# Moving the tiles that TensorE reads by 1 KB in SBUF: a decoder layer in split float32 on one core

## The chip, the cores and the metric

The kernel runs on one core of one Trainium2 chip. The metric is the device time of one execution in microseconds, taken as the median of several runs. The engines are called as in the profile: PE is TensorE's matmul stream, PEld its weight loads (LDWEIGHTS), DVE is VectorE, ACT is ScalarE, POOL is GpSimd, and SP issues the DMAs.

## The reference

One decoder layer over 512 tokens of width 2048, in float32. Three token mixers run on the same normalised input, their outputs go through one output projection, and a SwiGLU feed-forward follows. Each has a residual add, and a last RMSNorm ends it. What matters here is the second half:

```python
x = x + jnp.concatenate([ya, yb, yc], axis=-1) @ w_out[l]
h = rmsnorm(x, ffn_norm[l])
x = x + (jax.nn.silu(h @ w_gate[l]) * (h @ w_up[l])) @ w_down[l]   # 2048 -> 5632 -> 2048
return rmsnorm(x, final_norm)
```

## The kernel before

**Split operands.** Every large product is made in the fp32r type with both operands split into a high part (`hi`, a rounded copy) and a low part (`lo`, the rest). A product of two such operands is three matmuls (`mm3`, line 292): high by high, high by low, low by high. A matmul has a stationary operand of 128 columns, which LDWEIGHTS loads, and a moving operand of 256 or 512 columns (1 or 2 KB in each partition).

**Phase 1** (up to about 970 us) makes the input projection and the three mixers. Its matmul groups carry the names of their PSUM tiles: `pf`, `pq`, `pig`, `pvs`, `pcq`, `pk` and so on are projections; the rest is attention and the gated recurrence. `po` and `pp` are the output projection.

**Phase 2** begins with the last columns of the output projection, whose weights stay resident in `wo` tiles (groups `bt<-wo,mT`). Then comes the feed-forward: 44 chunks (22 of gate and 22 of up columns, 256 columns each). Each chunk is made by a scheme of seven products, `P1` to `P7`, each of 8 steps, and a step is two matmuls (lines 1337 and 1338). The high weights meet 512 moving columns, and the low weights meet 256:

```python
mm(ps, hi[:, q], v.rearrange("p k h t -> p (k h t)"), first and q == 0, False, skip_group_check=True)
mm(ps[:, :256], lo[:, q], v[:, 0, 0], False, q == 7, skip_group_check=True)
```

In the trace a product shows as 16 matmuls that alternate, for instance `Xg<-A,w` (512 columns) and `Xg<-A,lo` (256). The moving tile is `A` for P1 and P4 (groups X) and P2 (group V), and `S` for the others: P5 uses S1 and P3 uses S4 (both in group Z), P6 uses S2 and P7 uses S3 (both in group X, so `Xg<-S` and `Xu<-S` are always S2 or S3). From the second block on, each chunk also carries a piece of the down projection of the block before: four steps of 12 matmuls (`fd<-w,aT`, 512 columns), put between the products by line 1449:

```python
ORDER = ("P1", "d", "P5", "d", "P6", "P2", "d", "P7", "d", "P4", "d", "P3")
```

40 of the 44 chunks have such `d` steps (39 in this order, the last one in a similar one). The kernel ends with the last piece of the down projection, `bt<-wl`.

**Places in SBUF.** Tiles come from pools that lie one behind the other in each partition, in the order of lines 117 to 121 and 1113: `const`, `big`, `slots`, `raws`, `rings`, and then `cb`, `ysp`, `wk` in phase 1, in whose place `fp` lies in phase 2. The sizes in `const` decide where all that follows begins, and `fp` began with the 64 bytes of `s4`. Counted from the start of a 2 KB block, the built program puts them here:

```
tiles                                                   before   after
big, slots, rings: hT, mT, A11 A12 A22 S1, S4, aT, w      160     1184   (moved by 1024)
fp: wo, S2, S3, lo (the low weights)                      224     1184   (moved by  960)
fp: xq, hf (not read by a large product)                  480     1440   (moved by  960)
ysp: w0, split inputs of the attention                   1088       64   (moved by 1024)
const: ident                                             1152     1152
```

All sizes of these tiles are multiples of 2 KB or 4 KB, so a 512-column moving operand always begins at the place in the table; a stationary operand of 512 bytes begins there or 512, 1024 or 1536 bytes further. Where a `w` tile holds two row blocks of 256 columns (`pf`, `pvs`), the second one begins 1024 bytes further.

Of the kernel before, what the change touches and what calls it, by code (L numbers as in the profile page):

```python
# [31 lines left out]
F32 = mybir.dt.float32  # L32
# [8 lines left out]
P = 128  # L41
T = 512
NT = T // P
# [64 lines left out]
def tile_hymba(ctx: ExitStack, tc: tile.TileContext, x, attn_norm, w_in, q1, k1, q2, k2, da_norm, hg_norm,  # L108
# [8 lines left out]
    const = ctx.enter_context(tc.tile_pool(name="const", bufs=1))  # L117
# [8 lines left out]
    def slot(name):  # L126
        return slots.tile([P, 1024], F32, name=name, tag="slot")
# [64 lines left out]
    sp.dma_start(ident, ctab[:, C_ID:C_ID + P])  # L192
    mhalf = const.tile([P, 4], F32, name="mhalf")
    pool.memset(mhalf, -0.5)

    def rstd_of(dst, ss, n, dim):

        pool.tensor_scalar(dst, ss, 1.0 / dim, EPS, op0=ALU.mult, op1=ALU.add)
        pool.tensor_tensor(dst, dst, mhalf[:, :n], op=ALU.pow)
# [911 lines left out]
    with ExitStack() as p2:  # L1111
        hurry[0] = False
        fp = p2.enter_context(tc.tile_pool(name="fp", bufs=1))
        s4 = fp.tile([P, NT, 4], F32, name="s4")
        gain2 = [slot(f"gain2{hf}") for hf in range(2)]
        for hf in range(2):
            sp.dma_start(gain2[hf], bcast_row(ffn_norm[0:1, hf * 1024:(hf + 1) * 1024], 1024))
# [418 lines left out]
```

## Time and profile before

| | |
|---|---|
| time, median of 3 runs | 2404.65 us (2404.49 to 2404.81) |
| time of the profiled execution | 2403.6 us |
| its span, first to last instruction | 2401.8 us |
| mean granted TensorE clock | 0.997 |

The span is what the views of the trace cover; the profiled execution took 1.8 us more than its span, and 1.05 us less than the median. The records of consecutive matmuls overlap, since a matmul drains while the next one streams. So the duration in a record (some 390 ns for 512 columns) is not what a matmul costs; its cost is the time from its start to the next start.

### The profile page before, as it was taken

The page shows a single profiled execution, that of the slowest core. Times are in us where ns is not written, and L with a number is a line of the kernel's source. Part 1 is how long each engine was busy: PE and PEld are TensorE (multiplying, and loading weights), DVE is VectorE, ACT ScalarE, POOL GpSimd, SP SyncE. Part 2 cuts the span into 40 slices and gives each one's busy share as a digit, 9 for nine tenths or more (in the row PEclk, how much of TensorE's full clock was granted, in tenths as well). Part 3 has the DMA queues.
Part 4 walks back from the last instruction along what each step waited for, and adds up shares of the span by engine and source line. Part 5 has one row for each costly group of instructions (what it writes and reads, how often), then busy time and mean ns, then how long its engine had stood idle before and what let it go on. Part 6 is the DMA issues. An engine that isn't in the chain of part 4 may idle for free.

```text
span 2401.8 us, 32892 instructions
## 1 busy us (share of the span) xinstructions
PE 2361.2 (98%) x12720; PEld 2019.1 (84%) x12720; DVE 1584.2 (66%) x2472; ACT 1032.5 (43%) x1800; POOL 50.3 (2%) x85
## 2 busy tenths in 40 slices
PE   9999999999999999979999999999999999999998
PEld 7898888898888778768888888888888888888887
DVE  6355556543656574687777777777777777777785
ACT  5343443443434443454444444444444444444452
POOL 2000000000000000000000000000000000000001
PEclk9999999999999999999999999999999999999999
DMA  6322222443221422534555555565555555555553
GB/s 207 97 73 80 65 82 81 137 131 100 62 62 53 144 81 74 179 101 122 191 187 190 190 190 193 193 193 193 193 193 193 191 187 188 188 193 192 189 187 150
DMA packets 355888, 354.17 MB, mean 147 GB/s; under 512 B 12882, under 2 KB 286738, under 8 KB 355732
## 3 DMA queue, kind: packets, MB, share of 16 engines
q1 hardware_dynamic: 355732, 352.07, 45.9%
q8 instruction: 100, 1.64, 0.3%
q14 instruction: 56, 0.46, 0.1%
HBM read 302.74 MB, written 49.28 MB: 147 GB/s over the span
## 4 chain that ended last, share of the span: by engine, by line
PE 94%; DVE 3%; ACT 1%; DMA 1%; issue 1%; POOL 0%; SPq 0%; ACTq 0%; POOLq 0%; DVEq 0%
PE fd L145 18%; PE Xu L145 10%; PE Xg L145 10%; PE pig L145 6%; PE po L145 5%; PE Zg L145 5%; PE Zu L145 5%; PE pq L145 3%; PE pf L145 3%; PE pcq L145 3%; PE Vg L145 2%; PE Vu L145 2%; PE bt L145 2%; PE pak L145 2%; PE pk L145 2%; PE sc L145 2%
## 5 line engine op out<-in xcount | busy, mean ns | idle before, releaser
L202 ACT ACTIVATE w<-raw 128x512 fp32r<-128x512 f32 (+2 forms) x698 | 549.0, 790 | 926.7 <-PE fd L145 148.4
L203 DVE TENSOR_TENSOR w<-raw,w 128x512 fp32r<-128x512 f32 (+1 forms) x432 | 293.8, 681 | 343.5 <-ACT w L202 340.4
L145 PE MATMUL fd<-w,aT 128*128 128x512 f32 x1920 | 467.6, 392 | 0.0
L203 DVE TENSOR_TENSOR lo<-raw,w 128x1024 fp32r<-128x1024 f32 x266 | 323.3, 1223 | 179.0 <-ACT w L202 179.0
L145 PEld LDWEIGHTS fd<-w,aT 128*128 128x128 f32 x1920 | 348.9, 188 | 75.3
L1260 DVE TENSOR_TENSOR raw<-raw,raw 128x1024 f32<-128x1024 f32 x134 | 163.4, 1219 | 6.8 <-DMA raw<-in_w_gate_dram 3.2
L145 PE MATMUL pig<-w,hT 128*128 128x512 f32 x576 | 138.3, 395 | 0.0
L145 PE MATMUL po<-w,mT 128*128 128x512 f32 x576 | 136.1, 393 | 0.0
L145 PE MATMUL Xu<-A,w 128*128 128x512 f32 x352 | 125.7, 396 | 1.5 <-DVE C L1346 1.5
L145 PE MATMUL Xg<-A,w 128*128 128x512 f32 x352 | 125.6, 396 | 1.3 <-DVE C L1346 1.3
L145 PE MATMUL Zg<-S,w 128*128 128x512 f32 x352 | 124.2, 392 | 1.7 <-DVE S L1233 1.7
L145 PEld LDWEIGHTS po<-w,mT 128*128 128x128 f32 x576 | 106.8, 188 | 21.5
L145 PEld LDWEIGHTS pig<-w,hT 128*128 128x128 f32 x576 | 106.2, 188 | 21.3
L145 PE MATMUL Zu<-S,w 128*128 128x512 f32 x352 | 124.2, 392 | 0.0
L145 PE MATMUL Xu<-S,w 128*128 128x512 f32 x352 | 123.0, 391 | 0.6 <-ACT C L1343 0.6
L145 PE MATMUL Xg<-S,w 128*128 128x512 f32 x352 | 122.8, 390 | 0.0
L1403 DVE TENSOR_TENSOR xq<-xq,fd 128x512 f32<-128x512 f32 x156 | 100.1, 683 | 0.3
L145 PE MATMUL Xg<-A,lo 128*128 128x256 f32 x352 | 99.1, 281 | 0.0
L145 PE MATMUL Xu<-A,lo 128*128 128x256 f32 x352 | 99.1, 281 | 0.0
L145 PE MATMUL Zg<-S,lo 128*128 128x256 f32 x352 | 98.4, 280 | 0.0
L145 PE MATMUL Zu<-S,lo 128*128 128x256 f32 x352 | 98.4, 280 | 0.0
L145 PE MATMUL Xg<-S,lo 128*128 128x256 f32 x352 | 97.6, 277 | 0.0
(344 smaller groups left out, 4324.8 us busy)
## 6 DMA issues: line engine op xcount, KB each, us to landing
raw<-in_w_gate_dram SPq DMA_DIRECT2D x112, 512.0 KB, 4.6
raw<-in_w_up_dram SPq DMA_DIRECT2D x112, 512.0 KB, 4.6
raw<-in_w_down_dram SPq DMA_DIRECT2D x88, 512.0 KB, 5.2
raw<-in_w_in_dram SPq DMA_DIRECT2D x80, 512.0 KB, 3.5
xq<-y SPq DMA_DIRECT2D x78, 512.0 KB, 4.9
y<-xq SPq DMA_DIRECT2D x78, 512.0 KB, 2.7
raw<-in_w_out_dram SPq DMA_DIRECT2D x32, 512.0 KB, 3.6
raw<-in_w_in_dram SPq DMA_DIRECT2D x48, 256.0 KB, 3.1
```

The source lines that it names most:

```text
L145: return pe.matmul(o, l, r, start=start, stop=stop, **kw)
L202: act.activation(hi, src, AF.Copy)
L203: dve.tensor_tensor(lo, src, hi.bitcast(F32), op=ALU.subtract)
L1260: dve.tensor_tensor(self.raw[out], self.raw[a], self.raw[b], op=ALU.subtract)
L1403: dve.tensor_tensor(o, o, ps[tt], op=ALU.add)
```

## The change

`s4`, which the squares of the rows are summed into, is taken from the pool `const` and no longer from `fp`, and a tile of 960 bytes that nothing uses is added to `const`. `const` grows by 64 + 960 = 1024 bytes, and the tiles move as in the table above. The built program has the same instructions in the same order on every engine, with the same semaphores and the same values waited for. Only addresses differ.

```diff
@@ -192,6 +192,9 @@
     sp.dma_start(ident, ctab[:, C_ID:C_ID + P])
     mhalf = const.tile([P, 4], F32, name="mhalf")
     pool.memset(mhalf, -0.5)
+    s4 = const.tile([P, NT, 4], F32, name="s4")
+
+    const.tile([P, 240], F32, name="room")
 
     def rstd_of(dst, ss, n, dim):
 
@@ -1111,7 +1114,6 @@
     with ExitStack() as p2:
         hurry[0] = False
         fp = p2.enter_context(tc.tile_pool(name="fp", bufs=1))
-        s4 = fp.tile([P, NT, 4], F32, name="s4")
         gain2 = [slot(f"gain2{hf}") for hf in range(2)]
```

## Rows read from the trace of the kernel before

**Rows 1.** The page: busy time, granted clock by slice, the chain by engine.

```profile
PE 2361.2 (98%) x12720; PEld 2019.1 (84%) x12720; DVE 1584.2 (66%) x2472; ACT 1032.5 (43%) x1800; POOL 50.3 (2%) x85
...
PEclk9999999999999999999999999999999999999999
...
PE 94%; DVE 3%; ACT 1%; DMA 1%; issue 1%; POOL 0%; SPq 0%; ACTq 0%; POOLq 0%; DVEq 0%
```

**Rows 2.** Waits of PE: total us, times, longest us.

```profile
PE hpsA L1225 <- DVE A L1233: 7.8, 3, 3.2
PE hpsS L1225 <- DVE S L1233: 6.1, 3, 3.8
PE pt L962 <- DVE pr L930: 4.0, 3, 1.8
```

**Rows 3.** Chain in order of time, one chunk: start us, us, matmuls.

```profile
1506.23 2.77 PE fd L145 x12
1509.00 2.74 PE Xg L145 x16
1511.74 2.78 PE Vg L145 x16
1514.52 2.77 PE fd L145 x12
1517.29 2.74 PE Xg L145 x16
1520.03 2.74 PE fd L145 x12
1522.78 2.77 PE Xg L145 x16
1525.55 2.77 PE Zg L145 x16
1528.32 2.77 PE Xu L145 x16
1531.09 2.77 PE fd L145 x12
...
1561.49 0.70 PE fd L145 x3
```

**Rows 4.** Busy time by engine in that chunk, PE clock, DMA share, GB/s.

```profile
1500.50:1530.90 30.40, 30.40 (x162) 26.10 (x161) 23.15 (x28) 13.71 (x18) 0.00 (x0) 1.00 0.59 191
```

**Rows 5.** Chain, a 512-column stage of phase 1.

```profile
69.93 43.52 PE pig L145 x192
```

**Rows 6.** Chain, the kernel's last stage.

```profile
2349.91 43.53 PE bt L145 x192
```

**Rows 7.** Chain, a 256-column stage of phase 1.

```profile
471.78 5.74 PE pvs L145 x48
```

**Rows 8.** Timeline, PE: an earlier 256-column stage, and what follows it.

```profile
42.05 5.91 PE L145 MATMUL pf<-w,hT 128*128 128x256 f32 x48
47.80 0.40 PE L145 MATMUL pq<-hT,w 128*128 128x512 f32 x1
```

**Rows 9.** Timeline, PE: steps of a product with S2.

```profile
1510.22 0.39 PE L145 MATMUL Xg<-S,w 128*128 128x512 f32 x1
1510.45 0.28 PE L145 MATMUL Xg<-S,lo 128*128 128x256 f32 x1
1510.56 0.39 PE L145 MATMUL Xg<-S,w 128*128 128x512 f32 x1
```

**Rows 10.** Timeline, PEld: the weight loads in a product's first steps.

```profile
1503.30 0.19 PEld L145 LDWEIGHTS Zg<-S,lo 128*128 128x128 f32 x1
1503.53 0.19 PEld L145 LDWEIGHTS Zg<-S,w 128*128 128x128 f32 x1
```

**Rows 11.** Timeline, PE: the matmuls of the same two steps.

```profile
1503.30 0.39 PE L145 MATMUL Zg<-S,w 128*128 128x512 f32 x1
1503.53 0.28 PE L145 MATMUL Zg<-S,lo 128*128 128x256 f32 x1
```

**Rows 12.** Timeline, PE: output projection with resident weights, and what follows.

```profile
997.30 14.68 PE L145 MATMUL bt<-wo,mT 128*128 128x512 f32 x63 [1.28 <-issue]
1011.82 1.03 PE L1225 MATMUL hpsA<-ident,hf 128*128 128x128 f32 x8
```

**Rows 13.** Chain, products of the first block, behind a stall.

```profile
1085.32 2.83 PE Zg L145 x16
1088.14 2.83 PE Zu L145 x16
1090.97 2.83 PE Xg L145 x16
1093.80 2.83 PE Zg L145 x16
1096.62 2.80 PE Xg L145 x16
```

## Prediction

> **What bounds the kernel now.** I read the page first: PE is busy for 98% of the span, the chain that ended last is PE for 94%, and the clock stands at its upper level (2.4 GHz) in every slice [rows 1]. Then the waits: the longest total that PE waited for anything is 7.8 us [rows 2]. So the time is, nearly, the sum of the steps from one matmul's start to the next. Since the change leaves order, semaphores and shapes alone, it can act only through the length of such a step. The view for that is the chain in order of time, which gives whole runs of equal matmuls. In the feed-forward it shows nothing but PE, eleven pieces for a chunk: seven products and four `fd` pieces. From the first `fd` piece of one chunk to that of the next it is 1561.49 - 1531.09 = 30.40 us [rows 3], and PE is busy for all of such a window [rows 4].
>
> The reader should see that these pieces are not equal. A product has 16 matmuls, eight of each width. It takes 2.77 us with A and in group Z, and 2.74 us where `Xg` stands behind an `fd` piece for P6 and P7, which read S2 and S3. The `fd` pieces take 2.77 us, except 2.74 us behind the second of these [rows 3]. Shape, clock and cover are the same; what differs is the place of the tiles: S2 and S3 begin at 224, the A tiles, S1 and S4 at 160. So place does count here, by about 1%.
>
> How can it? A weight load starts together with the matmul ahead of it: the load for `Zg<-S,lo` starts at 1503.30 with the matmul `Zg<-S,w`, and the next load at 1503.53 with the matmul `Zg<-S,lo` [rows 10, 11]. So two reads of SBUF run at once, a moving operand and the following weights, and I take it (it is not shown) that they disturb each other by the distance between their places. In S2 and S3 steps that distance is 224 to 224 in the 512-column matmul and 224 to 160 in the 256-column one; in the others it is 160 to 224 and 160 to 160.
>
> The Trainium skill says otherwise ("TensorE: Matmul & The Clock Gate", Step-by-step: what each phase is for): "Loading the next tile's weights doesn't steal SBUF read bandwidth from the running matmul." By that sentence addresses cannot matter and the change is worth 0. The trace does not agree with it in full: 2.74 against 2.77 us for matmuls of the same shapes [rows 3].
>
> **The change part by part.** The removed and added lines issue no instruction of their own; `s4` keeps its writers and readers. What is left is two moves.
>
> *The shift by 1 KB that all share.* It leaves every distance between `big`, `slots` and `rings` as it was. What it could alter is where an operand crosses a 2 KB boundary. For weights the trace has the answer: a stage's four token tiles load from 160, 672, 1184 and 1696 in turn, the last one across the boundary; after the change the same four places come in another order. For 256 moving columns too: in `pvs` every second group of 12 begins at 160 and at 1184, and a matmul takes 5.74/48 = 119.6 ns [rows 7]; in the `pf` stage three quarters begin at 1088 or 64, the rest at 160, and it takes (47.80 - 42.05)/48 = 119.8 ns [rows 8]. I price this move at 0. Moving operands of 512 columns at 1184 are in no row; that stays a rival below. Other engines and DMA move with their tiles; in the chunk DVE is busy for 23.15 and ACT for 13.71 of 30.40 us, and DMA for 0.59 [rows 4], so even some per cent there stay hidden.
>
> *The shift by 960 bytes of the `fp` tiles.* It brings S2, S3, `wo` and `lo` to the same place as the rest. All pairs then are 1184 to 1184. Stages in which all operands already stand alike give the price: 512 columns take 43.52/192 = 226.7 ns in `pig` and 43.53/192 = 226.7 ns in the last stage [rows 5, 6], 256 columns take 119.6 ns [rows 7]. Eight steps of one each are 8 x 346.3 ns = 2.77 us. That is what products with A, S1 and S4 take now, so I leave these at 2.77. The others follow:
> - S2 and S3 products: 2.74 to 2.77, two in a chunk: +0.06 us.
> - the `fd` piece behind the second one: 2.74 to 2.77: +0.03 us.
> - `Vg<-A` behind the first one, now 2.78 [rows 3], to 2.77: -0.01 us.
> - that is +0.08 us in a chunk, and 40 chunks have it: +3.2 us. The four chunks of the first block have eight such products without `fd`: 8 x 0.03 = +0.2 us.
> - `bt<-wo` has 224 against 160 now: (1011.82 - 997.30)/63 = 230.5 ns [rows 12]. With all alike 226.7 ns; 96 of them: -0.4 us.
>
> Sum: +3.0 us. The profiled execution took 2403.6 us, 2401.8 of it span, and 1.05 us less than the median of the runs; with the sum it becomes 2406.6 us, and against the median 2407.7 us, +0.12%.
>
> The pair of a 512-column step and a 256-column step in one place is in no row, so both ends are kept. Low end: each step as short as the shortest steady one. A step pair of S2 takes 1510.56 - 1510.22 = 0.34 us [rows 9], eight are 2.72 us; twelve `fd` matmuls at 226.7 ns are 2.72 us. Eleven pieces of 2.72 are 29.92 against 30.40 us [rows 4]: -0.48 us, in 40 chunks -19.2 us. High end: right behind a stall in the first block, products with the very same tiles ran at 2.83 us, four in a row [rows 13]. So a pair can settle at more than one length. Seven products at 2.83 and four `fd` pieces at 2.77 are 30.89 us: +0.49 us, in 40 chunks +19.6 us. I take the value between, since the stages with one place are nearest to the new state, and since it is what most products show now.
>
> **The rivals.**
> - *All pairs fall into the short step* (faster). For it: both steady 512-column stages with one place, 226.7 ns, have the length that S2's steps have too, and `fd` pieces would then enter in step and lose their 2.77. Against it: 256 columns in one place take 119.6 ns, where S2's 256-column step takes 1510.56 - 1510.45 = 0.11 us [rows 9]. -19.2 us: 2385.5 us.
> - *All pairs settle in the long step* (slower). For it: rows 13 show it, and the first `fd` matmuls behind a product with one place are those that make that piece longer than 12 x 226.7 ns = 2.72 us. Against it: it came only behind a stall, and the chain shows 2.77 for the same tiles 40 chunks long. It decides if the load of `lo`, now moved from 64 bytes beside the moving operand to its very place, costs the 512-column step 7 ns more. +19.6 us: 2424.3 us.
> - *Nothing changes at all* (same). Then the 2.74 us would come from the order of the products and not from places. For it: P6 and P7 always stand behind `fd` in the chain. Against it: so does P4, with 2.77 [rows 3]. 2404.7 us. The sentence of the Trainium skill quoted above would have this outcome.
> - *The 2 KB boundary counts for 512 columns*, which the operand now crosses at its column 216 and not 472. If it costs or saves one such step of 6.7 ns (the difference of 2.77 and 2.72 over eight pairs), the program's 7500 matmuls with 512 columns make 50 us either way: 2455 or 2354 us. No row speaks for it; rows 7 and 8 speak against.
>
> **How the numbers follow.** My forecast 0.42; all short 0.16; all long 0.19; nothing 0.10; boundary 0.03 faster and 0.04 slower; the rest, 0.06, is a mixture of product kinds with half of either end. A measurement of this kernel tells about 0.2% (4.8 us) from no change. The forecast, 2404 to 2411 us in its own range, lies within that for nine parts in ten; with "nothing changes" this makes same 0.38 + 0.10 = 0.48. Faster: 0.16 + 0.03 + 0.03 = 0.22. Slower: 0.19 + 0.04 + 0.03 + 0.04 = 0.30. The range takes in both ends of the pair and leaves out the boundary: 2385 to 2425 us.
>
> **What would show it.** In the chain of the changed kernel: `Xg<-S` at 2.77 us and the `fd` behind it at 2.77; `Vg<-A` at 2.77; `pig` and the last stage at 43.5 us; `pvs` at 119.6 ns; `bt<-wo` at 226.7 ns. If A products leave 2.77, the pair settles elsewhere, and it should do so in all seven products of a chunk and in all chunks alike. If `pig` or the last stage leave 43.5 us, the common shift by 1 KB counts, and my first price is wrong.

## Result, and the profile of the changed kernel

The changed kernel takes 2420.66 us (median of 4 runs, 2415.63 to 2423.57) against 2404.57 us (4 runs). The ratio is 1.0064, 95% interval 1.0049 to 1.0078: slower by 0.64%, or 16 us. The profiled execution is the quickest of the four, 2415.63 us with a span of 2413.8 us.

The page (busy time, granted clock by slice, the chain by engine) and the waits of PE (total us, times, longest us) answer to [rows 1, 2]:

```profile
PE 2375.0 (98%) x12720; PEld 2020.3 (84%) x12720; DVE 1584.8 (66%) x2472; ACT 1031.2 (43%) x1800; POOL 50.8 (2%) x85
...
PEclk9999999999999999999999999999999999999999
...
PE 94%; DVE 3%; ACT 1%; DMA 1%; issue 1%; POOL 1%; SPq 0%; ACTq 0%; POOLq 0%; DVEq 0%
```

```profile
PE hpsS L1227 <- DVE S L1235: 6.0, 3, 3.8
```

PE has 13.8 us more busy time in the same 12,720 matmuls, in a span that is 12.0 us longer. The longest total wait is 6.0 us, where it was 7.8. So the time lies in the steps themselves. The chain in order of time (start us, us, matmuls), first the stages of phase 1, then one chunk, then the last stage:

```profile
69.76 43.52 PE pig L145 x192
...
471.60 5.74 PE pvs L145 x48
...
1533.92 2.73 PE fd L145 x12
...
1539.46 2.78 PE fd L145 x12
1542.24 2.81 PE Xu L145 x16
1545.05 2.83 PE Vu L145 x16
1547.88 2.75 PE fd L145 x12
...
1553.44 2.78 PE fd L145 x12
...
1564.69 2.73 PE fd L145 x12
...
2361.93 43.53 PE bt L145 x192
```

`pig`, `pvs` and the last stage take as long as they did, to the hundredth [rows 5 to 7]. In a chunk every product is longer: 2.81 us behind an `fd` piece and 2.83 us behind another product, where it was 2.74 to 2.78 [rows 3]. The four `fd` pieces went both ways, 2.73 to 2.78 where they were 2.74 or 2.77, and their sum stays, 11.04 us for 11.05. The chunk takes 1564.69 - 1533.92 = 30.77 us against 30.40: +0.37 us, in 40 chunks +14.8 us (counting all of them as equal to this one). Over it the clock is full and PE is never idle (columns as in [rows 4]):

```profile
1533.92:1564.69 30.77, 30.77 (x161) 26.14 (x161) 21.74 (x27) 12.62 (x16) 0.00 (x0) 1.00 0.57 187
```

The timeline of PE shows a product with S2 again, to set against [rows 9]:

```profile
1511.99 0.40 PE L145 MATMUL Xg<-S,w 128*128 128x512 f32 x1
...
1513.05 0.40 PE L145 MATMUL Xg<-S,w 128*128 128x512 f32 x1
```

The two starts are three pairs apart, which take 1513.05 - 1511.99 = 1.06 us, 0.353 us each, where a pair with S2 took 0.34. From the same view, `bt<-wo` takes (1009.12 - 994.73)/63 = 228.4 ns a step [rows 12]:

```profile
994.73 14.55 PE L145 MATMUL bt<-wo,mT 128*128 128x512 f32 x63 [0.49 <-issue]
1009.12 1.03 PE L1227 MATMUL hpsA<-ident,hf 128*128 128x128 f32 x8
```

### The profile page after: what moved, and what is told of

Its sections match the earlier page's. It is cut to its first block, busy times and chain, and to the rows that moved or that the text cites. A ratio compares the mean times of both kernels' runs of the same rounds, so it can differ in the third digit from the quotient of the medians.

```text
span 2413.8 us, 32892 instructions
## 1 busy us (share of the span) xinstructions
PE 2375.0 (98%) x12720; PEld 2020.3 (84%) x12720; DVE 1584.8 (66%) x2472; ACT 1031.2 (43%) x1800; POOL 50.8 (2%) x85
## 4 chain that ended last, share of the span: by engine, by line
PE 94%; DVE 3%; ACT 1%; DMA 1%; issue 1%; POOL 1%; SPq 0%; ACTq 0%; POOLq 0%; DVEq 0%
PE fd L145 18%; PE Xu L145 10%; PE Xg L145 10%; PE pig L145 5%; PE po L145 5%; PE Zg L145 5%; PE Zu L145 5%; PE pq L145 3%; PE pcq L145 3%; PE Vg L145 3%; PE Vu L145 2%; PE pf L145 2%; PE bt L145 2%; PE pak L145 2%; PE pk L145 2%; PE sc L145 2%
## 5 line engine op out<-in xcount | busy, mean ns | idle before, releaser
L145 PE MATMUL Xu<-S,lo 128*128 128x256 f32 x352 | 98.7, 280 | 0.0
```

What stands on the lines that cost most here:

```text
L145: return pe.matmul(o, l, r, start=start, stop=stop, **kw)
```

## Experiments

Two theories. **Distance:** a step's length depends on how far, within a block of 512 bytes, the moving operand lies from the weights loaded meanwhile; the change took the distance of `lo`, S2 and S3 to zero. **Place:** the shift by 1 KB that all tiles share does it. In the edits, P is 128 and a float32 column is 4 bytes, so a pad of 112 columns is 448 bytes and one of 16 columns is 64. Where a run is compared with the kernel before, that ran on the same chip. Chunk lengths are taken from the first `fd` piece of an up chunk to that of the next chunk, as above.

### The distance alone, and the shift alone

`e1_no_room` is the changed kernel without the room, so all tiles stand at 224 in a 512-byte block:

```diff
     s4 = const.tile([P, NT, 4], F32, name="s4")
-    const.tile([P, 240], F32, name="room")
```

> Only the distance is closed, without the shift by 1 KB: s4 moves to the first pool and nothing else is added, so hi, lo, the residuals' tiles and all other operands start 224 bytes into a 512-byte block. Theory 'distance' (the bytes between the start of what streams and of what is loaded next, within 512 bytes, set the pace): products of a chunk at 2.81 us behind fd and 2.83 us behind another product, as in the changed kernel, time 2415 to 2424 us. Theory 'place' (the shift by 1 KB does it): products stay at 2.77 and 2.74 us, time 2404.6 us.

`e2_room_only` is the kernel before with 1,024 bytes of room; `s4` stays in `fp`:

```diff
     pool.memset(mhalf, -0.5)
+    const.tile([P, 256], F32, name="room")
```

> Only the shift by 1 KB, without closing the distance: 1,024 bytes of room in the first pool, s4 stays where it was, so everything is moved by 1,024 bytes and lo, S2 and S3 stay 64 bytes beside hi. Theory 'distance': as the kernel before, A, S1 and S4 products 2.77 us, S2 and S3 products 2.74 us, time within 0.1% of 2404.6 us. Theory 'place': products 2.81 to 2.83 us, time 2415 to 2424 us.

Measured: `e1_no_room` 2421.55 us against 2404.56, ratio 1.0070 (1.0058 to 1.0083); `e2_room_only` 2403.59 us, ratio 0.9998 (0.9989 to 1.0007). The chain of each, first without the room, then with the room alone:

```profile
1536.38 2.83 PE Xu L145 x16
1539.21 2.73 PE fd L145 x12
...
1569.98 0.23 PE fd L145
```

```profile
1533.70 2.77 PE fd L145 x12
...
1542.01 2.74 PE Xu L145 x16
...
1564.11 2.77 PE fd L145 x12
```

The chunk takes 1569.98 - 1539.21 = 30.77 us without the room and 1564.11 - 1533.70 = 30.41 us with the shift alone. The whole effect comes with the distance. The shift by 1 KB is worth nothing that can be seen here (0.11% at the most, either way), and so is the crossing of a 2 KB boundary by a 512-column operand: the A tiles, S1, S4 and the `w` tiles cross it at the same column as in the changed kernel. Nor does a common shift by 64 bytes count: within 512 bytes all these tiles stand at 224 without the room and at 160 in the changed kernel, and the chunk takes 30.77 us in both.

### Which tile

`e3_lo_moved` moves only `lo`, by 448 bytes (a second pad keeps the tiles behind it in step), and `e4_s_moved` only S2, S3 and `wo`:

```diff
+        fp.tile([P, 112], F32, name="pad1")
         g, u = chunks(0, 0, both=True), chunks(0, 1, both=True)
```

```diff
         s4 = fp.tile([P, NT, 4], F32, name="s4")
+        fp.tile([P, 112], F32, name="pad1")
...
+        fp.tile([P, 16], F32, name="pad2")
         g, u = chunks(0, 0, both=True), chunks(0, 1, both=True)
```

> Of the kernel before, lo alone is moved, by 448 bytes, so that it stands at 160 in a 512-byte block like hi and A; S2, S3 and wo stay at 224. Theory 'distance': the products of A, S1 and S4 (5 of 7 in a chunk) go to 2.81 to 2.83 us, about +0.05 us x 200 = +8 to +10 us; those of S2 and S3 (what streams is now 64 bytes beyond both lo and hi) are not known from any row, 2.74 us if only the distance to hi counts there, up to 2.83; time 2409 to 2420 us. Rival 'the moving operand's own place counts, not what is loaded meanwhile': nothing changes, 2404.6 us.

> Of the kernel before, S2, S3 and wo alone are moved, to 160 in a 512-byte block like A and hi; lo stays at 224. Theory 'distance': S2 and S3 products take on the pace of A's, 2.742 to 2.77 us, fd behind them 2.745 to 2.767 us: 80 products x 0.03 = +2.4 us, fd up to +0.8 us more, time 2406.5 to 2408.5 us, the term of the prediction that was priced at +3. Rival 'S2 and S3 are quicker for another reason than their place (the stretch of the order they are in)': they stay at 2.74 us, 2404.6 us.

Measured: `e3_lo_moved` 2418.45 us, ratio 1.0061 (1.0048 to 1.0073); `e4_s_moved` 2408.74 us, ratio 1.0014 (1.0005 to 1.0023). The chain of each, `lo` first:

```profile
1538.16 2.73 PE fd L145 x12
...
1546.48 2.80 PE Xu L145 x16
1549.28 2.82 PE Vu L145 x16
...
1568.90 1.14 PE fd L145 x5
```

```profile
1532.95 2.77 PE fd L145 x12
...
1541.26 2.77 PE Xu L145 x16
1544.03 2.77 PE Vu L145 x16
...
1563.43 2.77 PE fd L145 x12
```

With S2, S3 and `wo` moved, every piece is 2.77 us and the chunk 1563.43 - 1532.95 = 30.48 us: +0.08 us, x 40 = +3.2 us. That is what the prediction had for this move in the chunks. The medians are 4.2 us apart, and the time lies just above the 2406.5 to 2408.5 us expected. With `lo` moved the chunk takes 1568.90 - 1538.16 = 30.74 us, +13.6 us in 40 chunks. So nearly all of the loss hangs on the place of `lo`, against the unmoved A tiles as well as S2 and S3. Those are now 64 bytes from `lo` and from `hi`, and they went to 2.80 us, a case that no row had shown before.

### Moving hi instead: distances of 64, 256, 128 and 32 bytes

If distance is the cause, there is a better choice than either kernel. `e5_hi_64_below` gives all seven products the relation that S2 and S3 had: the long step at distance 0 to `lo`, the short one 64 bytes from `hi`. A ring tile gets 4,608 bytes, and the chunks' `hi` sits at byte 448 of it. It starts from the changed kernel without the room; the row of ones moves out of `const` to free 512 bytes:

```diff
+    def ring(name, at=0):
+        return rings.tile([P, 1152], F32R, name=name, tag="ring")[:, at:at + 1024]
...
-                        w = rings.tile([P, 2, 512], F32R, name=f"w{uid[0]}", tag="ring")
+                        w = ring(f"w{uid[0]}").rearrange("p (h n) -> p h n", h=2)
...
-        ones = const.tile([1, P], F32, name="ones")
+        ones = wk.tile([1, P], F32, name="ones")
...
-                hi = rings.tile([P, 1024], F32R, name=f"w{uid[0]}", tag="ring")
+                hi = ring(f"w{uid[0]}", 112)
```

The others differ from it in that last number alone: 64 in `e6_hi_256_away`, 16 in `e7_hi_64_above`, 96 in `e10_hi_128_below`, 120 in `e11_hi_32_below`.

> A version meant to beat both kernels: in a chunk hi starts 64 bytes before lo, A and S within 512 bytes (ring tiles of 4,608 bytes, hi at byte 448 of one, fd's and the projections' weights at byte 0), so that all seven products stand as S2 and S3 did in the kernel before: the long step loads lo from the place of what streams, the short step loads hi from 64 bytes before it. The other operands of the large stages stand at one place. s4 moves as in the change, without its room; the 512-byte row of ones goes to the first phase's pool for space. Theory 'distance': all products 2.74 us, fd behind them 2.745 us, so 200 x 0.03 us of products and about 115 x 0.022 us of fd fall from the kernel before, 2404.6 - 6 - 2.5 = about 2396 us (2392 to 2399). Rival 'only the absolute place of S2 and S3 made them quick': products stay at 2.77 to 2.83 us, time 2404 to 2422 us.

> As the version with hi 64 bytes before, but hi stands 256 bytes from lo, A and S within 512 bytes. Theory 'any distance relieves the short step': 2.74 us per product, about 2396 us. Rival 'the sign or the closeness counts': products 2.77 to 2.83 us, 2404 to 2422 us.

> As the version with hi 64 bytes before, but hi stands 64 bytes beyond lo, A and S. Theory 'any distance relieves the short step': 2.74 us per product, about 2396 us. Rival 'the load must start at a lower place than what streams': products as in the changed kernel or longer, 2.81 to 2.83 us or more, 2415 us or more.

> As the version with hi 64 bytes before, at 128 bytes. If the pace repeats every 128 bytes, products at 2.81 to 2.83 us as at 0 and 256, 2416 to 2421 us; if it repeats every 256 bytes, 128 is as far away as can be: 2.72 to 2.74 us, 2391 us.

> As the version with hi 64 bytes before, at 32 bytes. If places are told apart by 64-byte pieces, half of each piece still meets its own: products between 2.73 and 2.82 us, 2391 to 2418 us; if a shift of 32 bytes is enough, 2.72 to 2.74 us, 2391 us; if it is nothing, 2.81 to 2.83 us, 2416 us or more.

The chain of `e5_hi_64_below`, of one chunk:

```profile
1527.92 2.74 PE fd L148 x12
...
1536.14 2.73 PE Xu L148 x16
1538.88 2.72 PE Vu L148 x16
...
1558.00 2.74 PE fd L148 x12
```

Of those with `hi` 64 bytes above, 256 and 128 bytes away, and 32:

```profile
1532.05 2.74 PE fd L148 x12
...
1562.13 2.74 PE fd L148 x12
```

```profile
1535.12 2.73 PE fd L148 x12
...
1565.89 2.73 PE fd L148 x12
```

```profile
1537.38 2.75 PE fd L148 x12
...
1568.08 2.07 PE fd L148 x9
```

```profile
1531.89 2.75 PE fd L148 x12
...
1562.18 2.75 PE fd L148 x12
```

| `hi` from `lo`, A and S | time, us | ratio to before (95%) | chunk, us | (chunk - 30.40) x 40 |
|---|---|---|---|---|
| 0 (`e1_no_room`) | 2421.55 | 1.0070 (1.0058 to 1.0083) | 30.77 | +14.8 |
| 256 | 2417.95 | 1.0057 (1.0044 to 1.0070) | 1565.89 - 1535.12 = 30.77 | +14.8 |
| 128 below | 2417.68 | 1.0061 (1.0047 to 1.0074) | 1568.08 - 1537.38 = 30.70 | +12.0 |
| 32 below | 2401.31 | 0.9991 (0.9982 to 1.0000) | 1562.18 - 1531.89 = 30.29 | -4.4 |
| 64 above | 2393.59 | 0.9955 (0.9942 to 0.9967) | 1562.13 - 1532.05 = 30.08 | -12.8 |
| 64 below | 2390.98 | 0.9942 (0.9930 to 0.9955) | 1558.00 - 1527.92 = 30.08 | -12.8 |

128 and 256 bytes count almost like 0; 64 bytes up or down is best, and 32 is in between. So neither "any distance" nor "only a lower place" holds. These six places fit a period of 128 bytes, and not the 512 of the first theory; no other distance was run. `e5_hi_64_below` beats the kernel before by 0.58%. Its 2390.98 us lie below the 2392 to 2399 expected, since the products fell to 2.72 to 2.74 us and not only to 2.74.

### Going further

`e8_rings_below` moves the whole ring pool 64 bytes below all else, by pads of 448 and 64 bytes around it, in the changed kernel without the room:

```diff
+    ctx.enter_context(tc.tile_pool(name="pad1", bufs=1)).tile([P, 112], F32, name="pad1")
     rings = ctx.enter_context(tc.tile_pool(name="rings", bufs=4))
+    ctx.enter_context(tc.tile_pool(name="pad2", bufs=1)).tile([P, 16], F32, name="pad2")
```

> The simple form: all ring tiles (hi of the chunks, fd's and the projections' weights) start 64 bytes before everything else within 512 bytes, by two pads of 448 and 64 bytes around their pool. Products as in the version with hi alone moved, 2.74 us. In fd and the projections what streams is now 64 bytes before what is loaded: if that is free in steps of 512 columns, as the long step of A's products was in the kernel before, fd stays at 2.745 us and a projection group at 43.52 us, time about 2396 us; if it costs 1 us in 43.5 us, as little as the bt group from wo paid for 64 bytes beyond (229.3 for 226.7 ns), fd's 1,900 steps alone give 5 us back, about 2401 us and more with the projections.

It takes 2401.69 us, ratio 0.9991 (0.9982 to 1.0000). The chain:

```profile
69.87 44.80 PE pig L147 x192
...
472.82 5.45 PE pvs L147 x48
...
1533.10 2.79 PE fd L147 x12
1535.88 2.73 PE Zu L147 x16
...
1563.34 2.79 PE fd L147 x12
```

The products have their 2.73 us, but `fd` pays 2.79 and `pig` 44.80/192 = 233.3 ns a step, where all stood at one place before and took 226.7. `pvs`, with 256 columns, gains instead: 5.45/48 = 113.5 ns, for 119.6. So in these two stages of equal steps, 512 columns did better at distance 0 and 256 columns at 64. The chunk (30.24 us) gives 6.4 us, of which 2.6 are left between the medians.

`e9_short_steps_too` uses that: `e5_hi_64_below`, with the weights of 256-column projections 64 bytes lower too.

```diff
-                        w = ring(f"w{uid[0]}").rearrange("p (h n) -> p h n", h=2)
+                        w = ring(f"w{uid[0]}", 112 if n == 256 else 0).rearrange("p (h n) -> p h n", h=2)
```

> The version with hi 64 bytes before, and the weights of the projections of 256 columns (pf and pvs) moved 64 bytes before hT as well; those of 512 columns stay at one place with it. Theory: in steps of 512 columns one place is best, in steps of 256 columns a distance of 64 bytes; with all rings moved, pf went from a mean of 124.8 to 120.6 ns and pvs from 119.8 to 116.7: 576 x 4.2 ns + 192 x 3.1 ns = -3.0 us on the 2391.0 us of the version without it, 2388 us. Rival: phase 1 there waits for loads or engines other than TensorE, and nothing is won, 2391 us.

It takes 2390.29 us, ratio 0.9949 (0.9937 to 0.9962), where 2388 us were expected. In the chain `pvs` gains, but less than with all rings moved, though its distances are the same: 5.65/48 = 117.7 ns a step.

```profile
469.96 5.65 PE pvs L148 x48
```

On the whole it can't be told from `e5_hi_64_below` (0.9942 against 0.9949, the intervals overlap): inconclusive.

## Why the prediction was right and wrong

**Right: PE's steps bound the kernel.** The waits kept their size in the changed kernel, and in each run whose time moved, the pieces of the chain moved the same way.

**Right: the shift by 1 KB is worth 0.** `e2_room_only` did it alone: ratio 0.9998, a chunk of 30.41 us. The rival of the 2 KB boundary falls with it. (Its own sum was slightly off: 2.77 - 2.72 us over eight pairs is 6.3 ns and not 6.7, and 47 us in all, not 50. Nothing else used it.)

**Right in itself: the +3.2 us for S2, S3 and the `fd` behind them.** `e4_s_moved` made just that move and shows each piece as forecast, `Xu` 2.77, `fd` 2.77, `Vu` 2.77 us. For `bt<-wo`, 226.7 ns were forecast and 228.4 came (from 230.5), so 0.2 us were gained there and not 0.4.

**Wrong: "That is what products with A, S1 and S4 take now, so I leave these at 2.77."** This is the term that was mis-sized, and it was sized at 0. Their `lo` moved too, from 64 bytes beside the moving tile to its very place, and they went from 2.77 to 2.81 and 2.83 us. S2 and S3 followed them there instead of stopping at 2.77. `e3_lo_moved` shows the cause: `lo` alone brings 0.34 of the 0.37 us that a chunk grew by. So the forecast of 2407.7 us, 2404 to 2411 in its own range, was 13 us short.

The argument behind the term was a sum of two stages of equal steps, 226.7 + 119.6 = 346.3 ns for a step pair, and it agreed with the 2.77 us of the A products. But that sum prices a pair at distances 0 and 0, and the A products stood at 64 and 0. With the equal steps that `e8_rings_below` shows (233.3 and 113.5 ns at 64 bytes), all four cases can be set side by side:

| long step, short step | 8 x (sum of equal steps) | product measured |
|---|---|---|
| 0, 0 (the changed kernel) | 8 x 346.3 = 2.77 us | 2.81 to 2.83 |
| 64, 0 (A before, `e4_s_moved`) | 8 x 352.9 = 2.82 us | 2.77 |
| 0, 64 (S2 and S3 before, `e5_hi_64_below`) | 8 x 340.2 = 2.72 us | 2.72 to 2.74 |
| 64, 64 (S2 and S3 in `e3_lo_moved`) | 8 x 346.8 = 2.77 us | 2.80 |

The sum holds for the third case and is off, to either side, for the others. A mixed sequence has a pace of its own, and agreement of the sum with the A products was chance. The growth is in the long step: by the start times of the timeline behind 1140 us, the step with 512 columns of the X products with A went from 229.6 to 235.6 ns on average, the one with 256 columns from 117.1 to 116.7. Nor are the pairs of the changed kernel alike: they take 350, 361 and 349 ns in turn, where those with A took 346 and 348 before, and those with S2 a steady 340 once settled.

**The rival that came true** is "all pairs settle in the long step", chance 0.19 and 2424.3 us. Its condition was met: with `lo` at the place of the moving operand the long step grew by 6 ns, where it had 7. It was a little too long, since products behind `fd` settle at 2.81 and the `fd` pieces take 11.04 us in a chunk and not 4 x 2.77: 14.8 us in 40 chunks where it had 19.6. The change is slower by more than 0.2%, which had 0.30. The range, 2385 to 2425 us, holds the time because that rival's row of before, [rows 13], was taken as its upper end. That was in part luck: the Z products of those rows stood at distances 64 and 0, so their 2.83 us was another pace of the old state and no measurement of the new one.

**What the size does not cover.** The medians are 16.1 us apart, the two profiled executions 12.0 us in their spans. The first `fd` piece of the kernel before, of the changed kernel, and of `e1_no_room` with its last stage:

```profile
1135.89 2.77 PE fd L145 x12
```

```profile
1133.81 2.78 PE fd L145 x12
```

```profile
1139.10 2.78 PE fd L145 x12
...
2367.86 43.53 PE bt L145 x192
```

From there to the last stage the changed kernel takes 2361.93 - 1133.81 = 1228.12 us and `e1_no_room` 2367.86 - 1139.10 = 1228.76 us, against 2349.91 - 1135.89 = 1214.02 us: +14.1 and +14.7 us, about what the chunks give. Ahead of it the one is 2.1 us early and the other 3.2 us late, at the same distances. So the rest lies there, where two executions can be 5.3 us apart; whether a part of it belongs to the distances stays open. In the first block the changed kernel also showed a run of products at the short pace behind a stall, where the kernel before showed the long one [rows 13], with the granted clock at 1.00 in both:

```profile
1083.06 2.77 PE Zg L145 x16
1085.83 2.77 PE Zu L145 x16
```

So at one and the same distance a sequence can settle at more than one pace, and the table above holds for the chunks with `fd` alone. What sets the pace, and why these places matter so, no run settles. In the products it also stays open whether the distance of `hi` from `lo` counts by itself: all products of the chunks at 2.80 us or more have `hi` and `lo` a multiple of 128 bytes apart, those at 2.72 to 2.78 us have them 32 or 64 apart, and each run that changed this changed the distance of one of them from the moving tile too. That the moving operand's distance counts is shown by the products at 2.77 and 2.72 us, whose `hi` and `lo` are equally far apart, and by `pig` in `e8_rings_below`.

**The sentence of the Trainium skill** that the prediction weighed ("TensorE: Matmul & The Clock Gate", Step-by-step: what each phase is for), that loading the next weights doesn't steal read bandwidth from the running matmul, does not hold in full for this kernel, if it is read to mean that the place of those weights cannot matter. With order, shapes and instructions of the feed-forward unchanged, the place of `hi` alone moved the ratio to the kernel before from 0.9942 (`e5_hi_64_below`) to 1.0070 (`e1_no_room`). The bandwidth itself no run measures. The Trainium skill also says that PE never waits on anyone for SBUF ("SBUF — State Buffer", SBUF: two separate sides). No run here shows PE waiting for another engine's access; what these runs add is that the length of PE's step depends on the places of its own two operands.

## What to carry to other kernels

When PE is busy throughout and its pieces of equal shape differ by a per cent, tabulate for each the start of the moving operand and of the weights loaded under it, modulo 128 bytes, before looking at anything else. In the alternating steps of 512 and 256 columns of this kernel the best was: the weights loaded under the long step at distance 0, those under the short step at 64. A small tile put in or taken out ahead of the operands can cost or give half a per cent through that alone; so a price taken from stages of equal steps holds for a mixed sequence only if a run shows it.

## What the runs showed of the hardware that was not expected

- The length of a step of fp32r matmuls depends on the distance between what streams and the weights loaded meanwhile: 226.7 ns at 0 and 233.3 ns at 64 bytes for 512 columns, 119.6 and 113.5 to 117.7 ns for 256. In the chunks' products distances of 0, 128 and 256 bytes acted nearly alike (30.77, 30.70 and 30.77 us a chunk), as with a period of 128.
- The preference was opposite for the two widths, and two equal distances in an alternating pair (0 and 0, 64 and 64, so that `hi` and `lo` stand at one place) were the slowest in the chunks, 2.80 to 2.83 us per product.
- The paces last: a chunk's pieces repeat. Behind a stall the same products were seen at another pace. Even the best version, `e5_hi_64_below`, ran through part of its first block at 2.80 us:

```profile
1086.70 2.80 PE Zg L148 x16
```

- Executions of one kernel differ by up to 8 us, and the quicker ones tend to have the higher mean granted clock: among the 21 of the kernel before that ran beside `e1_no_room`, the quickest took 2401.00 us at 0.998 and the slowest 2407.57 us at 0.994. The clock fell in the first block, where PE stands still between products: from 1029.77 to 1034.20 us, behind 3.70 us in which PE was busy for 1.28, the kernel before had a mean clock of 0.63, so it ran at the lower level (1.2 GHz) for most of that time (columns as in [rows 4]):

```profile
1026.00:1029.70 3.70, 1.28 (x8) 1.16 (x9) 3.56 (x6) 1.31 (x3) 0.00 (x0) 1.00 0.19 71
1029.77:1034.20 4.43, 4.43 (x20) 3.80 (x19) 3.71 (x6) 0.89 (x3) 1.71 (x2) 0.63 0.16 59
```
